# A combination written over its own source, paired residual loads and stores on SyncE in a one-core encoder layer

## The chip, the core and the metric

The kernel runs on one core of one Trainium2 chip. The metric is the device time of one launch in microseconds. The kernel before takes 855.76 us (median of three runs, 854.52 to 856.06). The engines are named as the profile names them: PE (TensorE matmul; PEld is its weight load), DVE (VectorE), ACT (ScalarE), POOL (GpSimd) and SP (SyncE, which here only issues DMAs). SPq and POOLq are the instruction streams of SP and POOL.

## The reference, cut to what matters

The reference is one encoder layer on x of 1024 positions by 1024 channels: a Fourier token mixer, then a gated MLP with a 3-tap convolution over positions, each with adaLN modulation before it and a residual and LayerNorm behind it.

```python
h = modulate(x, sh1, sc1)
y = fourier_mixer(h, w_out)                      # real part of fft2, then a linear map
x = layer_norm(ALPHA * x + g1 * y, mix_g, mix_b) # kept in HBM as x1d

h = modulate(x, sh2, sc2)
u = h @ w_up                                     # 1024 -> 2 * 2816
u = conv3_over_positions(u) + conv_b
val, gate = u[:, :2816], u[:, 2816:]
y = (gelu(gate) * val) @ w_down                  # 2816 -> 1024
x = layer_norm(ALPHA * x + g2 * y, ffn_g, ffn_b) # the output
```

All tensors are float32.

## The kernel before, in words

Every large matmul is done three times (`hl3`, L282 to L285): both operands are split into a high part (ACT, L52) and a low part (DVE, L53, the source minus its high part), and high times high, high times low and low times high are added in PSUM. So each matmul operand costs one ACT and one DVE instruction before PE can use it.

**Up projection.** The 2816 value and 2816 gate columns are done in 22 blocks `j` of 128 and 128. Blocks 0 and 1 are done plainly (L570 to L620): block 1 has four accumulators `x1_{ph}{v}`, for the two halves `ph` of the positions and for value and gate, written in the order ph 0, then ph 1. From block 2 on, a block is done with seven instead of eight products (a Strassen-Winograd scheme, L624 to L669). On the side of the weights it needs the sums S1 to S4 of the four raw quarters, which POOL makes (L632 to L635) in the tiles `S12_j` (slot 31) and `S34_j` (slot 32). On the side of the positions it needs combinations T1 to T4 of the quarters `B` of the activations (`comb`, L531), made once by DVE and then split: T2 has its raw form in slots 46 and 47, and T4, which is T2 minus a quarter, has its raw form in slots 31 and 32. Slots 31 and 32 hold two weight tiles of block 0 before that, and `S12_2` and `S34_2` after that. T3 is split into the tiles `Hh0` to `Hh3`, over the positions 512 to 1023 of the plain operand, which block 1 reads at ph 1. The result of each block is convolved and gated (`gated`, L572) and stored to HBM (`gd`) by POOL.

**Down projection.** It also has seven products `p`, done in the order 1, 2, 5, 6, 3, 7, 4 (L915), each in six pieces `i` of the contraction: five pieces of two 128-row tiles and one single tile. The g operand of product `p` is read from `gd`, and the w operand from the weights; sums are made by DVE (L747, L762) or by DMAs from POOL that add to what is in the tile (L732, L752, L756). PE adds products in `o{p}_{m}{c}`, one bank for each 128-row block `m` of positions, and `evac` (L808) adds a finished product into the tiles `C[0]` (upper positions) and `C[1]` (lower positions).

**Upper rows.** After products 2 and 3 a half of the columns of the upper rows is complete. For each row block `m` and each half `h` of the columns, `upper_half` (L873) multiplies by the gate (L875) and adds the residual `xu`, a 128x512 piece of x1d that SP loads (`xu_load`, L794). There are two slots for it, 24 and 44, used in turn by m. `upper` and `normed` (L878, L883) then make the LayerNorm: ACT squares (L887), DVE and POOL make the inverse deviation (L423, L425), ACT scales (L891), DVE multiplies by `ffg` (L892) and adds `ffb` (L893), and `store` issues the DMA to the output, from POOL for the upper rows and from SP for the lower rows. The lower rows are done after products 7 and 4 (`lower`, L898, and L825 to L864).

**What sets the order.** PE, DVE and ACT instructions are put in order by the compiler's scheduler from its own estimate; SP and POOL (`manual_schedule`, L924) issue in the order in which the code is written. Every engine works strictly through its own list, so an instruction that waits holds up all behind it. `UL` (L921) says before which step (p, i) an `xu_load` is written, `U0` and `U1` where the halves of the upper rows are written, `XL` where the residual of the lower rows (`xf`) is loaded. Loads of operands run seven steps ahead (L926).

Of the kernel before, what the change touches and what calls it, by code (L numbers as in the profile page):

```python
# [8 lines left out]
F32 = mybir.dt.float32  # L9
F32R = mybir.dt.float32r  # L10
AF = mybir.ActivationFunctionType
ALU = mybir.AluOpType
# [23 lines left out]
def encoder_layer(ctx: ExitStack, tc: tile.TileContext, I, out: bass.AP):  # L36
# [8 lines left out]
    def slot(i, shape, dt, name):  # L45
        return big.tile([128] + list(shape), dt, tag=f"s{i}", name=name)
# [8 lines left out]
    def E(name):  # L55
        return pool if name in ON_POOL else dve
# [371 lines left out]
    for n_t, t in enumerate((1, 2, 0, 3)):  # L428
        ts_ = slice(128 * t, 128 * t + 128)
        xr = []  # L430
# [100 lines left out]
    def comb(name, x, y, op, sl):  # L531
        out_ = []
        for i in range(2):
            v = slot(sl + i, [2, 512], F32, f"{name}_{i}")
            for q in range(2):
                E(name).tensor_tensor(v[:, q, :], x[2 * i + q], y[2 * i + q], op)
                out_.append(v[:, q, :])
        return out_
# [67 lines left out]
    T3 = comb("T3", B[1, 1], B[0, 1], ALU.subtract, 34)  # L606
    T4 = comb("T4", T2, B[1, 0], ALU.subtract, 31)
    gated(0, u0[0], u0[1])
    u1 = [slot((2, 0)[v], [S], F32, f"u1_{v}") for v in range(2)]
    for ph in range(2):  # L610
        for v in range(2):
            g = slice(512 * ph, 512 * ph + 512)
            acc = xbank(f"x1_{ph}{v}")
            plain_mm(acc, a1, v, lambda a: a[:, g])
            act.activation(u1[v][:, g], acc, AF.Copy)
# [176 lines left out]
    xr = {}  # L792

    def xu_load(m, h):  # L794
        v = slot((24, 44)[m % 2], [512], F32, f"xu{m}_{h}")
        sp.dma_start(v, x1d[128 * m : 128 * m + 128, 512 * h : 512 * h + 512])
        xr[0, m, h] = v

# [5 lines left out]
    def store(half, m):  # L804
        r0 = 512 * half + 128 * m
        (pool, sp)[half].dma_start(out[r0 : r0 + 128, :], C[half][m])

# [75 lines left out]
    def normed(half, m, nmu):  # L883
# [9 lines left out]
        E(f"ub{m}").tensor_tensor(c, c, ffb, ALU.add)  # L893
        store(half, m)

# [24 lines left out]
    XL = {(7, 5): (1, 0), (4, 0): (1, 1), (4, 1): (1, 2), (4, 2): (1, 3)}  # L920
    UL = {**{(6, i): (i - 1, 0) for i in range(1, 5)}, **{((7, i) if i else (3, 5)): (i, 1) for i in range(4)}}  # L921
    U0 = {(6, i + 1): i - 1 for i in range(1, 5)}
    U1 = {(7, i + 1): i for i in range(4)}
    ctx.enter_context(tc.manual_schedule(engines={mybir.EngineType.SP, mybir.EngineType.Pool}))  # L924
    for n, (p, i) in enumerate(steps):
# [37 lines left out]
        while split_n < min(len(steps), n + 2):  # L963
            opnd[steps[split_n]] = operands(*steps[split_n], ready.pop(steps[split_n]))
            split_n += 1
        late.append((PAIRS[i], opnd.pop((p, i))))
        if (p, i) in U1:
            upper_half(U1[p, i], 1)
            upper(U1[p, i])
# [122 lines left out]
```

## Time and profile before

| what | value |
|---|---|
| time, three runs | 854.52, 855.76, 856.06 us |
| the profiled execution: time | 853.01 us |
| the profiled execution: span | 851.1 us |
| PE busy (share of the span) | 797.7 us (94%) |
| DVE busy | 702.5 us (83%) |
| ACT busy | 387.0 us (45%) |
| POOL busy | 244.5 us (29%) |
| mean granted clock of PE | 0.976 |
| HBM read, written | 110.39 MB, 19.92 MB |

The span goes from the first to the last instruction of the profiled execution, which is 1.9 us less than that execution's own time; that in turn is 2.75 us below the median of the three runs. The up projection's seven-product blocks fill about 232 to 614 us, the down projection 614 to 830 us, and from 830 us on only LayerNorm and stores are left. In a timeline row the first two numbers are start and duration in us, then engine, line, operation, output<-inputs; in square brackets stands how long the engine sat idle before it and what ended that.

### The profile page before, as it was taken

The page shows a single profiled execution, that of the slowest core. Times are in us where ns is not written, and L with a number is a line of the kernel's source. Part 1 is how long each engine was busy: PE and PEld are TensorE (multiplying, and loading weights), DVE is VectorE, ACT ScalarE, POOL GpSimd, SP SyncE. Part 2 cuts the span into 40 slices and gives each one's busy share as a digit, 9 for nine tenths or more (in the row PEclk, how much of TensorE's full clock was granted, in tenths as well). Part 3 has the DMA queues.
Part 4 walks back from the last instruction along what each step waited for, and adds up shares of the span by engine and source line. Part 5 has one row for each costly group of instructions (what it writes and reads, how often), then busy time and mean ns, then how long its engine had stood idle before and what let it go on. Part 6 is the DMA issues. An engine that isn't in the chain of part 4 may idle for free.

```text
span 851.1 us, 10735 instructions
## 1 busy us (share of the span) xinstructions
PE 797.7 (94%) x3943; PEld 643.7 (76%) x3943; DVE 702.5 (83%) x1030; ACT 387.0 (45%) x559; POOL 244.5 (29%) x205
## 2 busy tenths in 40 slices
PE   2899999878999999999999999999999989999990
PEld 1566768667878888888888888888878878888880
DVE  7959677888799999998888888888677784557897
ACT  7634435565733444444444443444354334335611
POOL 2162013230064433444433334331000122702203
PEclk9999999988999999999999999999999999999995
DMA  9987843821113122222222222210598887988903
GB/s 343 363 296 244 327 171 124 322 100 49 50 58 116 74 87 108 102 76 75 75 94 82 97 87 87 74 50 25 200 376 301 270 229 127 193 159 237 292 26 124
DMA packets 50613, 133.90 MB, mean 157 GB/s; under 512 B 5608, under 2 KB 6760, under 8 KB 50560
## 3 DMA queue, kind: packets, MB, share of 16 engines
q1 hardware_dynamic: 39504, 103.59, 34.1%
q0 software_dynamic: 10768, 28.58, 13.7%
q10 hardware_dynamic: 288, 1.05, 0.3%
q8 instruction: 31, 0.51, 0.2%
q14 instruction: 22, 0.18, 0.1%
HBM read 110.39 MB, written 19.92 MB: 153 GB/s over the span
## 4 chain that ended last, share of the span: by engine, by line
PE 74%; DVE 11%; DMA 9%; issue 3%; ACT 2%; POOL 1%; SPq 0%; POOLq 0%; DVEq 0%; ACTq 0%
PE x L284 16%; PE x L285 16%; PE x L283 16%; PE o L284 4%; PE o L285 4%; PE o L283 4%; DMA xu<-x1d 4%; PE ada L135 2%; DMA gr<-gd 2%; DMA wd<-in_w_down_dram 1%; PE B L283 1%; DVE d_1l L53 1%; PE B L285 1%; PE B L284 1%; DVE d_0l L53 1%
## 5 line engine op out<-in xcount | busy, mean ns | idle before, releaser
L283 PE MATMUL x<-Hh,a 128*128 128x512 f32 (+2 forms) x416 | 157.3, 380 | 4.2 <-ACT Hh L52 4.2
L284 PE MATMUL x<-Hl,a 128*128 128x512 f32 (+2 forms) x416 | 157.0, 379 | 1.8 <-DVE Hl L53 1.8
L285 PE MATMUL x<-Hh,a 128*128 128x512 f32 (+2 forms) x416 | 155.7, 376 | 0.9 <-DVE a L53 0.9
L284 PE MATMUL o<-d_1l,d_0h 128*128 128x512 f32 (+1 forms) x299 | 114.8, 385 | 3.1 <-DVE d_1l L53 3.1
L285 PE MATMUL o<-d_1h,d_0l 128*128 128x512 f32 (+1 forms) x299 | 114.3, 384 | 0.0
L283 PE MATMUL o<-d_1h,d_0h 128*128 128x512 f32 (+1 forms) x299 | 102.8, 383 | 0.0
L283 PEld LDWEIGHTS x<-Hh,a 128*128 128x128 f32 x416 | 79.9, 193 | 19.6 <-ACT Hh L52 5.1
L284 PEld LDWEIGHTS x<-Hl,a 128*128 128x128 f32 x416 | 79.4, 191 | 18.1 <-DVE Hl L53 3.9
L285 PEld LDWEIGHTS x<-Hh,a 128*128 128x128 f32 x416 | 79.4, 191 | 15.1 <-DVE a L53 1.3
L52 ACT ACTIVATE a<-S 128x512 fp32r<-128x512 f32 x80 | 49.9, 628 | 85.4 <-PE x L285 70.5
L284 PEld LDWEIGHTS o<-d_1l,d_0h 128*128 128x128 f32 x299 | 56.7, 190 | 15.2 <-DVE d_1l L53 4.1
L285 PEld LDWEIGHTS o<-d_1h,d_0l 128*128 128x128 f32 x299 | 56.7, 189 | 10.9
L283 PEld LDWEIGHTS o<-d_1h,d_0h 128*128 128x128 f32 x299 | 56.2, 188 | 11.0
L53 DVE TENSOR_TENSOR a<-S,a 128x512 fp32r<-128x512 f32 x80 | 60.6, 758 | 2.8 <-ACT a L52 2.2
L53 DVE TENSOR_TENSOR a<-wu,a 128x512 fp32r<-128x512 f32 x60 | 62.1, 1037 | 0.0
L587 POOL DMA_DIRECT2D gd<-ug x20 | 11.5, 573 | 170.4 <-DVE ug L586 170.4
L52 ACT ACTIVATE a<-wu 128x512 fp32r<-128x512 f32 x60 | 37.3, 624 | 33.2 <-PE x L285 33.2
L634 POOL TENSOR_TENSOR S<-wu 128x512 f32<-128x512 f32 x20 | 28.1, 1406 | 63.1 <-DVE a L53 57.2
L578 DVE SCALAR_TENSOR_TENSOR t<-uv,cw,t 128x1023 f32<-128x1023 f32 x20 | 34.6, 1731 | 11.6 <-ACT t L577 11.5
L53 DVE TENSOR_TENSOR d_1l<-wd,d_1h 128x1024 fp32r<-128x1024 f32 (+1 forms) x37 | 44.0, 1189 | 0.0
L635 POOL TENSOR_TENSOR S<-wu,S 128x512 f32<-128x512 f32 x20 | 43.9, 2193 | 0.1
L52 ACT ACTIVATE d_0h<-Sg 128x1024 fp32r<-128x1024 f32 x15 | 15.9, 1061 | 56.6 <-PE o L284 56.6
(317 smaller groups left out, 1839.2 us busy)
## 6 DMA issues: line engine op xcount, KB each, us to landing
aw<-in_ada_w_dram SPq DMA_DIRECT2D x48, 512.0 KB, 6.8
wu<-in_w_up_dram SPq DMA_DIRECT2D x44, 512.0 KB, 3.2
gd<-ug POOLq DMA_DIRECT2D x20, 512.0 KB, 2.9
wd<-in_w_down_dram SPq DMA_DIRECT2D x20, 512.0 KB, 10.8
gr<-gd SPq DMA_DIRECT2D x15, 512.0 KB, 7.1
gA<-gd SPq DMA_DIRECT2D x10, 512.0 KB, 9.7
Sg<-gd POOLq DMA_DIRECT2D x10, 512.0 KB, 6.4
x<-in_x_dram SPq DMA_DIRECT2D x8, 512.0 KB, 7.3
```

The costliest lines, as they stand in the source:

```text
L52: act.activation(hi, src, AF.Copy)
L53: (eng or dve).tensor_tensor(lo, src, hi, ALU.subtract)
L135: pe.matmul(pm[32 * g : 32 * g + 32, :], cb[:, kt, :], ws[kt][:, q * g : q * g + q], start=(kt == 0), stop=(kt == KT - 1), tile_position=( ...
L283: pe.matmul(ps_ap, hi_l, hi_r, start=first, stop=False)
L284: pe.matmul(ps_ap, hi_l, lo_r, start=False, stop=False)
L285: pe.matmul(ps_ap, lo_l, hi_r, start=False, stop=last)
L578: dve.scalar_tensor_tensor(tt[:, 1:S], u[:, 0 : S - 1], w[:, 0:1], tt[:, 1:S], ALU.mult, ALU.add)
L587: pool.dma_start(gd[j], gg)
L634: pool.tensor_tensor(S3, A11, A21, ALU.subtract)
L635: pool.tensor_tensor(S4, A12, S2, ALU.subtract)
```

## The change

It has three parts.

1. T4 is written over T2's raw tiles (slots 46 and 47) instead of into slots 31 and 32 (`comb` with `None` as slot), and block 1 of the up projection does positions 512 to 1023 (ph 1) before 0 to 511 (ph 0).
2. The residual of the upper rows is loaded as four pieces of 256 rows by 512 columns (one DMA of 512 KB for two row blocks), not eight of 128 rows. Slot 24 has the row blocks 0 and 1, slot 44 the row blocks 2 and 3. `UL` puts the loads of the first column half at steps (2, 5) and (5, 0) instead of (6, 1) to (6, 4), and those of the second half at (3, 1) and (3, 2) instead of (3, 5) and (7, 1) to (7, 3).
3. The upper rows are stored by SP at steps (4, 0) to (4, 3), not by POOL behind each row's LayerNorm.

```diff
--- before.py
+++ after.py
@@ -531,10 +531,11 @@
     def comb(name, x, y, op, sl):
         out_ = []
         for i in range(2):
-            v = slot(sl + i, [2, 512], F32, f"{name}_{i}")
+            v = slot(sl + i, [2, 512], F32, f"{name}_{i}") if sl is not None else None
             for q in range(2):
-                E(name).tensor_tensor(v[:, q, :], x[2 * i + q], y[2 * i + q], op)
-                out_.append(v[:, q, :])
+                o = x[2 * i + q] if v is None else v[:, q, :]
+                E(name).tensor_tensor(o, x[2 * i + q], y[2 * i + q], op)
+                out_.append(o)
         return out_
 
     cw = cp.tile([128, NB, 2, 4], F32, name="cw")
@@ -604,10 +605,10 @@
     t_op("T2", 1, T2)
     t_op("T1", 0, T1)
     T3 = comb("T3", B[1, 1], B[0, 1], ALU.subtract, 34)
-    T4 = comb("T4", T2, B[1, 0], ALU.subtract, 31)
+    T4 = comb("T4", T2, B[1, 0], ALU.subtract, None)
     gated(0, u0[0], u0[1])
     u1 = [slot((2, 0)[v], [S], F32, f"u1_{v}") for v in range(2)]
-    for ph in range(2):
+    for ph in (1, 0):
         for v in range(2):
             g = slice(512 * ph, 512 * ph + 512)
             acc = xbank(f"x1_{ph}{v}")
@@ -791,10 +792,11 @@
     C = [[slot(c, [D], F32, f"C{hf}_{m}") for m, c in enumerate(sl)] for hf, sl in enumerate(((0, 1, 4, 5), (2, 6, 7, 3)))]
     xr = {}
 
-    def xu_load(m, h):
-        v = slot((24, 44)[m % 2], [512], F32, f"xu{m}_{h}")
-        sp.dma_start(v, x1d[128 * m : 128 * m + 128, 512 * h : 512 * h + 512])
-        xr[0, m, h] = v
+    def xu_load(q, h):
+        v = slot((24, 44)[q], [2, 512], F32, f"xu{q}_{h}")
+        sp.dma_start(v, x1d[256 * q : 256 * q + 256, 512 * h : 512 * h + 512].rearrange("(m p) n -> p m n", p=128))
+        for m in range(2):
+            xr[0, 2 * q + m, h] = v[:, m, :]
 
     def x_load(half, m):
         xr[half, m] = slot((24, 44, 47, 48)[m], [D], F32, f"xf{half}_{m}")
@@ -803,7 +805,7 @@
 
     def store(half, m):
         r0 = 512 * half + 128 * m
-        (pool, sp)[half].dma_start(out[r0 : r0 + 128, :], C[half][m])
+        sp.dma_start(out[r0 : r0 + 128, :], C[half][m])
 
     def evac(p, m, x):
         c0, c1 = C[0][m], C[1][m]
@@ -891,7 +893,6 @@
         act.activation(c, c, AF.Identity, scale=rs, bias=nb)
         E(f"ug{m}").tensor_tensor(c, c, ffg, ALU.mult)
         E(f"ub{m}").tensor_tensor(c, c, ffb, ALU.add)
-        store(half, m)
 
     st1 = []
 
@@ -918,7 +919,7 @@
     TAIL = {3: 2, 7: 2, 4: 4}
     acc, late = None, []
     XL = {(7, 5): (1, 0), (4, 0): (1, 1), (4, 1): (1, 2), (4, 2): (1, 3)}
-    UL = {**{(6, i): (i - 1, 0) for i in range(1, 5)}, **{((7, i) if i else (3, 5)): (i, 1) for i in range(4)}}
+    UL = {(2, 5): (0, 0), (5, 0): (1, 0), (3, 1): (0, 1), (3, 2): (1, 1)}
     U0 = {(6, i + 1): i - 1 for i in range(1, 5)}
     U1 = {(7, i + 1): i for i in range(4)}
     ctx.enter_context(tc.manual_schedule(engines={mybir.EngineType.SP, mybir.EngineType.Pool}))
@@ -964,6 +965,8 @@
             opnd[steps[split_n]] = operands(*steps[split_n], ready.pop(steps[split_n]))
             split_n += 1
         late.append((PAIRS[i], opnd.pop((p, i))))
+        if p == 4 and i < 4:
+            store(0, i)
         if (p, i) in U1:
             upper_half(U1[p, i], 1)
             upper(U1[p, i])
```

Line numbers of the changed kernel are one higher than before from L538 on, and two higher in the later functions.

**SP, where the down projection's product 5 begins.** `wd11` are the weights that product 6 needs, `xu` the residual pieces (row block or pair, then column half), `gr13` and later the g operand of product 7. Before:

```order
L686 DMA wd11_0_5778<-in_w_down_dram 128x2x512
L686 DMA wd11_2_5817<-in_w_down_dram 128x2x512
L686 DMA wd11_4_5852<-in_w_down_dram 128x2x512
L686 DMA wd11_6_5888<-in_w_down_dram 128x2x512
L686 DMA wd11_8_5924<-in_w_down_dram 128x2x512
L686 DMA wd11_10_5958<-in_w_down_dram 128x512
L796 DMA xu0_0_6026<-x1d_66 128x512
L796 DMA xu1_0_6062<-x1d_66 128x512
L796 DMA xu2_0_6100<-x1d_66 128x512
L796 DMA xu3_0_6138<-x1d_66 128x512
L694 DMA gr13_6204<-gd_67 128x2x512
```

With the change:

```order
L797 DMA xu0_0_5752<-x1d_66 128x2x512
L687 DMA wd11_0_5778<-in_w_down_dram 128x2x512
L797 DMA xu1_0_5781<-x1d_66 128x2x512
L687 DMA wd11_2_5819<-in_w_down_dram 128x2x512
L687 DMA wd11_4_5854<-in_w_down_dram 128x2x512
L687 DMA wd11_6_5890<-in_w_down_dram 128x2x512
L687 DMA wd11_8_5926<-in_w_down_dram 128x2x512
L687 DMA wd11_10_5960<-in_w_down_dram 128x512
L695 DMA gr13_6198<-gd_67 128x2x512
L695 DMA gr14_6238<-gd_67 128x2x512
L797 DMA xu0_1_6242<-x1d_66 128x2x512
```

The first pair now stands ahead of all six weight loads and the second ahead of five of them; the second column half stands behind the second of product 7's loads, where it stood behind the sixth (outside these rows).

**POOL, at the first seven-product block (j = 2).** `u0_1` is the gated result of block 0. Before:

```order
L587 DMA gd_67<-u0_1_1824 128x1024
L634 TENSOR_TENSOR S34_2_2348<-wu2_0_2343 128x512
L632 TENSOR_TENSOR S12_2_2347<-wu2_0_2343,wu2_1_2345 128x512
L633 TENSOR_TENSOR S12_2_2347<-S12_2_2347,wu2_0_2343 128x512
L635 TENSOR_TENSOR S34_2_2348<-wu2_1_2345,S12_2_2347 128x512
L632 TENSOR_TENSOR S12_3_2494<-wu3_0_2490,wu3_1_2492 128x512
```

With the change:

```order
L635 TENSOR_TENSOR S34_2_2346<-wu2_0_2341 128x512
L633 TENSOR_TENSOR S12_2_2345<-wu2_0_2341,wu2_1_2343 128x512
L634 TENSOR_TENSOR S12_2_2345<-S12_2_2345,wu2_0_2341 128x512
L588 DMA gd_67<-u0_1_1824 128x1024
L636 TENSOR_TENSOR S34_2_2346<-wu2_1_2343,S12_2_2345 128x512
L633 TENSOR_TENSOR S12_3_2492<-wu3_0_2488,wu3_1_2490 128x512
```

The store of block 0 was ahead of all four sums of block 2, and is now behind three of them.

**DVE, upper rows against the end.** `pg` is product 4's result times the gate, the first step of the lower rows' end; `C0_2` and `C0_3` are the last two upper row blocks. The part of the list in which the last of their instructions stood, before:

```order
L831 TENSOR_TENSOR pg0_6860<-o4_00_6708,g2_5146 128x512
L912 BN_STATS stl3_6828<-C1_3_5299 128x6 x2
L831 TENSOR_TENSOR pg1_6896<-o4_10_6709,g2_5146 128x512
L832 SCALAR_TENSOR_TENSOR C1_0_5296,stl0_6756<-pg0_6860,C1_0_5296 128x512
L892 TENSOR_TENSOR C0_3_5295<-C0_3_5295,ffg_6462 128x1024
L832 SCALAR_TENSOR_TENSOR C1_1_5297,stl1_6801<-pg1_6896,C1_1_5297 128x512
L834 TENSOR_SCALAR nmuf40_6864<-stl0_6756 128x1
L831 TENSOR_TENSOR pg2_6932<-o4_20_6710,g2_5146 128x512
L893 TENSOR_TENSOR C0_3_5295<-C0_3_5295,ffb_6464 128x1024
L834 TENSOR_SCALAR nmuf41_6900<-stl1_6801 128x1
L843 TENSOR_TENSOR pg3_6989<-o4_30_6711,g2_5146 128x256
```

Where all of the upper rows' last instructions stand with the change, between the splits for products 7 and 4 (`d7`, `d4`):

```order
L894 TENSOR_TENSOR C0_0_5290<-C0_0_5290,ffg_6456 128x1024
L53 TENSOR_TENSOR d7_0l3_6512<-gr16_6314,d7_0h3_6511 128x1024
L895 TENSOR_TENSOR C0_0_5290<-C0_0_5290,ffb_6458 128x1024
L53 TENSOR_TENSOR d7_1l3_6516<-wd00_6_5316,d7_1h3_6515 128x1024
L53 TENSOR_TENSOR d4_0l1_6700<-gA22_1_6452,d4_0h1_6699 128x1024
L894 TENSOR_TENSOR C0_1_5291<-C0_1_5291,ffg_6456 128x1024
L894 TENSOR_TENSOR C0_2_5292<-C0_2_5292,ffg_6456 128x1024
L894 TENSOR_TENSOR C0_3_5293<-C0_3_5293,ffg_6456 128x1024
L895 TENSOR_TENSOR C0_1_5291<-C0_1_5291,ffb_6458 128x1024
L53 TENSOR_TENSOR d7_0l4_6563<-gr17_6350,d7_0h4_6562 128x1024
L53 TENSOR_TENSOR d4_1l1_6704<-wd01_2_5382,d4_1h1_6703 128x1024
L895 TENSOR_TENSOR C0_2_5292<-C0_2_5292,ffb_6458 128x1024
```

The four instructions of `C0_2` and `C0_3` with `ffg` and `ffb`, two of which stood among the `pg` rows and two between product 7's end and them, now stand ahead of product 7's end.

## The prediction

> **What bounds the kernel now.** I read the page first: the span, and the busy tenths of the engines by slice of 21.3 us.
>
> ```profile
> span 851.1 us, 10735 instructions
> PE   2899999878999999999999999999999989999990
> DVE  7959677888799999998888888888677784557897
> PEclk9999999988999999999999999999999999999995
> ```
>
> PE is full from the second slice to the last but one, so time can be won only where PE is not full or its clock drops, and behind its last matmul. The view by stretches says how much that is at the three places that the change touches (PE, PEld, DVE, ACT and POOL busy with counts, then granted clock, DMA share, GB/s).
>
> ```profile
> 240.00:250.00 10.00, 9.10 (x41) 7.20 (x40) 10.00 (x12) 3.37 (x5) 5.64 (x4) 1.00 0.29 107
> 680.00:700.00 20.00, 17.74 (x71) 14.15 (x71) 17.42 (x25) 6.03 (x6) 3.77 (x4) 0.91 0.87 222
> 820.00:851.00 31.00, 10.51 (x60) 9.09 (x58) 26.77 (x51) 4.97 (x7) 8.13 (x7) 0.72 0.25 103
> ```
>
> So: 0.9 us without PE at 241, 2.3 us and a lower clock in product 5 of the down projection, and an end in which DVE works 26.8 of 31 us. The other holes of PE (the start, and 180 to 210) lie ahead of the first instruction that moves, and I leave them as they are.
>
> **Part 1, T4 over T2: +1.2 us.** Timelines of PE, POOL, ACT and SP around 240, and how long the `wu` loads of that stretch took to land:
>
> ```profile
> 240.33 0.39 PE L284 MATMUL x<-TT1l,a 128*128 128x512 f32 x1
> 241.62 0.50 PE L285 MATMUL x<-Hh,a 128*128 128x512 f32 x1 [0.90 <-DVE a L53]
> 233.17 1.53 POOL L634 TENSOR_TENSOR S<-wu 128x512 f32<-128x512 f32 x1 [5.85 <-ACT u L615]
> 237.12 1.67 POOL L632 TENSOR_TENSOR S<-wu,wu 128x512 f32<-128x512 f32 x1 [2.42 <-DVE TT4l L53]
> 238.87 2.14 POOL L633 TENSOR_TENSOR S<-S,wu 128x512 f32<-128x512 f32 x1
> 234.16 0.57 ACT L655 ACTIVATE p<-x 128x512 f32<-128x512 f32 x1
> 220.55 0.33 SPq L549 DMA_DIRECT2D wu<-in_w_up_dram  x1
> DMA to landing us min/median/max: 3.1/4.1/4.7
> ```
>
> POOL's sums for block 2 start at 233 and 237, because S34 and S12 take the slots that T4 leaves only when it is split. Matmuls stand 0.227 us apart where nothing waits, so the one at 241.62 should have come at 240.56: 1.1 us, and 0.1 more as the next ones run slower. With the change slots 31 and 32 are free when block 0's last weights are read. What is late next is the second half of block 2's weights, issued at 220.55: with 4.7 us it is there at 225.3, S1 and S2 (1.67 and 2.14) at 229.1, and their splits (0.6 on ACT and DVE each) at 230.4. PE finishes product 0 about 234.1 and wants the operand of product 1 from 231.8 on. S3 and S4 are made by 232.5, and PE wants them ten microseconds later. That leaves 1.4 us of cover. If the splits are held up by more (DVE is full here), a wait comes back. Ends: -0.5 and +1.2; I take 1.2. The T4 subtractions are as many as before, and the turned order of block 1 has the same matmuls; it lets T3's splits, which overwrite positions 512 to 1023, start before block 1 ends.
>
> **Part 2, the residual pairs, at product 5: +3.2 us.** PE, DVE and SP there:
>
> ```profile
> 686.39 1.07 PE L283 MATMUL o<-d_1h,d_0h 128*128 128x512 f32 x4
> 689.72 0.50 PE L284 MATMUL o<-d_1l,d_0h 128*128 128x512 f32 x1 [2.26 <-DVE d_1l L53]
> 696.01 1.07 PE L283 MATMUL o<-d_1h,d_0h 128*128 128x512 f32 x4
> 701.45 1.07 PE L283 MATMUL o<-d_1h,d_0h 128*128 128x512 f32 x4
> ```
>
> ```profile
> 673.94 1.22 DVE L747 TENSOR_TENSOR wd<-wd,wd 128x1024 f32<-128x1024 f32 x1 [0.64 <-DMA wd<-in_w_down_dram]
> 686.08 0.69 DVE L876 SCALAR_TENSOR_TENSOR C<-xu,C 128x512 f32<-128x512 f32 x1 [0.91 <-DMA xu<-x1d]
> 688.45 1.22 DVE L53 TENSOR_TENSOR d_1l<-wd,d_1h 128x1024 fp32r<-128x1024 f32 x1
> 667.27 4.28 SPq L686 DMA_DIRECT2D wd<-in_w_down_dram  x6
> 671.85 17.03 SPq L796 DMA_DIRECT2D xu<-x1d  x4
> wd<-in_w_down_dram SPq DMA_DIRECT2D x20, 512.0 KB, 10.8
> ```
>
> A piece takes PE 701.45 - 696.01 = 5.44 us; this one took 9.62, so the hole costs 4.2 us: 2.26 of waiting and 1.9 at a lower clock. DVE is late with `d_1l` because it waits 0.91 us for `xu` and has a full list. [...]
>
> With the change the first pair is issued where the first `wd` was, so it lands about when that did, 673.9, and does not hold DVE up. But the weights come later. From the first `wd` at 673.9 to the `xu` at 686.1 the loads brought 2.25 MB of weights and 0.25 MB of `xu`: 4.9 us per MB. The first `wd` follows one pair (0.5 MB): 676.3; the last follows both: 689.7. DVE can begin at 673.7, when product 2's first rows are done, and by its new order has 1.75 us of work ahead of the first `wd` (two of 0.6 per 128x512, one of 1.14 per 128x1024): ready 675.9, so it waits 0.4. From there to the end of `d_1l` are four instructions of 1.14 and ten of 0.6 and one more 1.14: 688.0, against PE's 687.5. Then it wants the last `wd` at 688.0, and gets it at 689.7; piece 3's `d_1l` ends at 693.8 where PE comes at 693.5. Left are 0.8 us of waits with a little slow clock: 4.2 - 1.0 = 3.2. The pair's own size has no row; loads of that size (`wu` above from 3.1 us on, `wd` 10.8 in the median) bound it, and give 4.2 and 0 here. The early load of the second half meets nobody: it takes the place of DMAs at 771 to 784.
>
> **Parts 2 and 3, the end: +3.3 us.** DVE's groups from 806 on, then its timeline and PE's:
>
> ```profile
> L892 DVE TENSOR_TENSOR C<-C,ffg 128x1024 f32<-128x1024 f32 x2 | 2.4, 1214 | 0.0
> L893 DVE TENSOR_TENSOR C<-C,ffb 128x1024 f32<-128x1024 f32 x2 | 2.4, 1210 | 0.0
> 778.12 0.69 DVE L876 SCALAR_TENSOR_TENSOR C<-xu,C 128x512 f32<-128x512 f32 x1 [4.91 <-DMA xu<-x1d]
> 806.08 0.68 DVE L823 TENSOR_TENSOR C<-C,o 128x512 f32<-128x512 f32 x1
> 846.23 1.28 DVE L863 SCALAR_TENSOR_TENSOR C<-C,rsf,ffb 128x1024 f32<-128x1024 f32 x1 [0.44 <-POOL rsf L850]
> 769.45 0.39 PE L283 MATMUL o<-d_1h,d_0h 128*128 128x512 f32 x1
> 802.62 0.39 PE L285 MATMUL o<-d_1h,d_0l 128*128 128x512 f32 x1
> ```
>
> Product 7 starts on PE at 769.45, and its first row block is complete at 803.0. DVE takes it at 806.1, 3.1 us late, since it lost 4.9 us at 773 to 778 waiting for `xu`. From 806.1 to 847.5 it works without a hole of over 0.5 us: the end is DVE's list, and the upper rows' last four instructions are in it. With the change `xu` is there long before, and the list has those four (4 x 1.14 = 4.6 us) ahead of product 7's end, where DVE waited. PE's new order has 12 more matmuls ahead of that end, half narrow (2.0 us): DVE starts at 805.0 in the old clock, 1.1 us sooner. One split of 1.14 comes into the stretch. And PE now waits for DVE in it: 18 instructions of 0.6 and four of 1.14 stand before product 4's piece 3 is split (15.4 us), and PE has matmuls for 12.0, so the first finished row of product 4 comes at 21.0 to 22.7 us (slow clock) where DVE is at 20.9. I take 1.2 for it. 4.6 + 1.1 - 1.1 - 1.2 = 3.3; ends 1 and 5.
>
> The stores go from POOL to SP at like cost (us from issue to landing at the line's end), and SP has nothing urgent behind them but the residual of the lower rows, which is used 15 us later. I cost them at nothing.
>
> ```profile
> out_dram<-C POOLq DMA_DIRECT2D x4, 512.0 KB, 3.0
> out_dram<-C SPq DMA_DIRECT2D x4, 512.0 KB, 2.6
> ```
>
> **A new wait in product 7: -1.0 us.** DVE now has the four small products with POOL's result (`nbfn`, L892 of the new kernel) ahead of splits that PE needs, and POOL has its own list ahead of them:
>
> ```profile
> 771.50 0.33 SPq L694 DMA_DIRECT2D gr<-gd  x1
> 777.68 0.88 POOL L732 DMA_DIRECT2D gr<-gd  x1 [7.24 <-DMA gr<-gd]
> 784.25 1.47 POOL L425 TENSOR_TENSOR rs_fn<-ve_fn,mhalf 128x1 f32<-128x1 f32 x1 [4.45 <-DVE ve_fn L423]
> 794.57 1.24 POOL L756 DMA_DIRECT2D wd<-in_w_down_dram  x1 [0.43 <-issue]
> 795.34 1.32 POOL L425 TENSOR_TENSOR rs_fn<-ve_fn,mhalf 128x1 f32<-128x1 f32 x1
> gr<-gd POOLq DMA_DIRECT2D x5, 512.0 KB, 17.4
> ```
>
> Before, POOL waited for the rows (4.45); now the rows wait for POOL. The last g load of product 7 is issued when DVE frees its slot, 2.7 us into the product (2.1 before), and lands 6.2 us later: 8.9. POOL then issues two DMAs and makes the first power by 11.1, and one more in each 2.1 us (a DMA and a power), the fourth 1.3 behind the third: 16.6. Behind it DVE has eleven instructions of 1.14 to the split of product 4's piece 1: 29.2. PE gets there after 128 matmuls, seven of them narrow: 28.3. I take 1.0 us of lost time; ends 0 and 2.5.
>
> **Rivals.** (a) *Weights late.* The six `wd` queue behind 1 MB of residual, and if they take 10.8 us each time rather than share the way they did, product 5 keeps its whole hole: part 2's 3.2 us are gone, 852.3. For it: the DMA share was 0.87 there. Against: the first pair replaces traffic that came just behind. [...] (b) *The end does not shrink.* The four moved instructions only push DVE's splits, DVE is late for product 7's end as before, and the last 3.3 us stay: 852.4. For it: with the moved instructions DVE's list in product 7 is longer, and waits for POOL stand in it. Against: it lost 4.9 us there before and still did nearly all of it. (c) *Slower.* The chain load, POOL, `nbfn`, DVE, PE: each microsecond by which the last g load lands later than 8.9 goes to PE in full. If it takes the 17.4 us of POOL's own `gr` transfers instead of 6.2, that is 11.2 us more: 860. It is slower than before from some 8.4 us on, so from a landing 14.6 us behind the issue. For it: all loads of product 4 now follow it without a pause. Against: they stand behind it in the queue. (d) *Nothing happens*: an edit that the list shows but another wait covers everywhere, 855.8. I see no such wait.
>
> **How the numbers follow.** 1.2 + 3.2 + 3.3 - 1.0 = 6.7 us. The profiled execution's 853.0 would become 846.3; the median of the runs lies 2.75 us above it, and 855.8 becomes **849.1**. Chances: the forecast (845 to 852) 0.64, (a) 0.12, (b) 0.13, (c) 0.07, (d) 0.04. Good ends of all terms together (1.2 + 4.2 + 5 - 0) would give 845.4, so the range begins at 845; it goes up to 854, where (a) and (b) alone are inside and (c), (d) and (a) with (b) are left out. A measurement of this kernel tells about 0.2% (1.7 us) from no change. Faster by more: the forecast, and most of (a) and (b): 0.82. Within: (d) and the rest of (a) and (b), 0.10. Slower: 0.08.
>
> **What would show it.** Right: no idle PE at 241 and POOL's first sum of block 2 near 216; product 5's piece under 6.5 us; DVE without a wait for `xu`; nothing with `ffg` on a C[0] tile behind product 7; the last matmul to the last DVE instruction 15 us or less, where it was 17. Wrong: `wd` named as what DVE waits for in product 5 with over 2 us (a), DVE starting product 7's end over 2 us behind PE (b), or waits of DVE for `rs_fn` of more than 8 us in all (c).

## The result and the profile after

The changed kernel takes 848.33 us (median of four runs, 848.1 to 850.46) where the kernel before takes 855.91 us in the runs beside it: ratio 0.9924, 95% interval 0.9903 to 0.9945, so 4.7 to 8.3 us less, 6.5 in the middle. Forecast were 849.1 us and 6.7 us less. The profiled execution took 848.1 us; its span and the busy tenths by slice:

```profile
span 846.3 us, 10731 instructions
PE   2899999878999999999999999999999999999983
DVE  6959778887999999888888888888678794557997
PEclk9999999997999999999999999999999999999997
```

The view by stretches, at the three places shown of before:

```profile
240.00:250.00 10.00, 10.00 (x46) 8.28 (x45) 10.00 (x13) 3.64 (x7) 3.71 (x3) 1.00 0.30 107
680.00:700.00 20.00, 19.56 (x85) 15.60 (x84) 18.44 (x26) 8.03 (x8) 4.51 (x4) 1.00 1.08 320
820.00:846.00 26.00, 12.29 (x64) 10.42 (x62) 19.68 (x39) 3.73 (x6) 5.08 (x4) 0.76 0.20 82
```

PE has no hole near 241 any more, 0.4 us instead of 2.3 in product 5, and is still at work after 830, where it had stopped. **Early.** POOL's first two sums of block 2, from its timeline; they started at 233 and 237 before:

```profile
216.53 2.40 POOL L635 TENSOR_TENSOR S<-wu 128x512 f32<-128x512 f32 x1 [21.32 <-PE x L285]
225.78 1.39 POOL L633 TENSOR_TENSOR S<-wu,wu 128x512 f32<-128x512 f32 x1 [6.84 <-DMA wu<-in_w_up_dram]
```

**Product 5.** PE's rows at the piece that took 9.62 us, and DVE's one wait there; then how long after their issue product 6's weights landed (the trace has the landing of four of the six), of before and (second fence) of the changed kernel:

```profile
685.90 1.07 PE L283 MATMUL o<-d_1h,d_0h 128*128 128x512 f32 x4
687.40 0.50 PE L284 MATMUL o<-d_1l,d_0h 128*128 128x512 f32 x1 [0.44 <-DVE d_1l L53]
692.08 1.07 PE L283 MATMUL o<-d_1h,d_0h 128*128 128x512 f32 x4
688.87 0.69 DVE L748 TENSOR_TENSOR wd<-wd,wd 128x512 f32<-128x512 f32 x1 [1.52 <-DMA wd<-in_w_down_dram]
```

```profile
DMA to landing us min/median/max: 10.5/12.5/12.9
```

```profile
DMA to landing us min/median/max: 13.0/16.1/16.6
```

The piece now takes 692.08 - 685.90 = 6.18 us, though the weights land 2.5 to 3.7 us later behind their issue than before: DVE waits for the last of them, behind the split that PE needs, and no longer for `xu`.

**The end.** DVE's and PE's rows of the changed kernel from product 7 on:

```profile
777.27 0.16 DVE L892 TENSOR_TENSOR nbfn<-nmufu,rs_fn 128x1 f32<-128x1 f32 x1 [3.33 <-POOL rs_fn L425]
801.97 0.69 DVE L825 TENSOR_TENSOR C<-C,o 128x512 f32<-128x512 f32 x1 [0.66 <-PE o L285]
813.63 0.28 PE L283 MATMUL o<-d_1h,d_0h 128*128 128x256 f32 x1
816.21 1.22 DVE L53 TENSOR_TENSOR d_1l<-wd,d_1h 128x1024 fp32r<-128x1024 f32 x1
817.48 0.50 PE L284 MATMUL o<-d_1l,d_0h 128*128 128x512 f32 x1 [3.57 <-DVE d_1l L53]
818.96 0.63 PE L283 MATMUL o<-d_1h,d_0h 128*128 128x512 f32 x1
821.93 0.40 PE L284 MATMUL o<-d_1l,d_0h 128*128 128x512 f32 x1
841.42 1.28 DVE L865 SCALAR_TENSOR_TENSOR C<-C,rsf,ffb 128x1024 f32<-128x1024 f32 x1
```

DVE is now at product 7's end before PE has it (0.66 us of waiting; it came 3.1 us late before). But in product 4 PE waits 3.57 us for a split, and the twelve matmuls behind it take 821.93 - 817.48 = 4.45 us, where 2.7 would do at the 0.227 us at which matmuls follow each other when nothing waits. So PE's last matmul comes at 832.0, 1.8 us later than before, and the time from there to DVE's last instruction falls from 17.3 to 10.7 us.

To compare kernels by stage, four landmarks serve, and only distances between them are compared: the last wait in the plain blocks of the up projection (202.22 before, 204.03 changed), the first matmul of product 1 (614.79, 615.18), product 5's pieces (above), and the row at which DVE takes product 6's first result, before and changed:

```profile
737.69 0.69 DVE L818 TENSOR_TENSOR C<-C,o 128x512 f32<-128x512 f32 x1 [2.89 <-PE o L285]
```

```profile
734.02 0.69 DVE L820 TENSOR_TENSOR C<-C,o 128x512 f32<-128x512 f32 x1 [2.89 <-PE o L285]
```

| stage, us | before | changed | less by | forecast |
|---|---|---|---|---|
| up to the plain blocks | 202.22 | 204.03 | -1.8 | 0 |
| from there to product 1 | 412.57 | 411.15 | 1.4 | 1.2 |
| products 1, 2 and half of 5 | 71.60 | 70.72 | 0.9 | 0 |
| product 5's two pieces | 15.06 | 11.88 | 3.2 | 3.2 |
| from product 6's first result to DVE's last instruction | 109.82 | 108.68 | 1.1 | 2.3 |

The rows add up to the 4.8 us between the two spans; the stretch between the fourth and the fifth row takes 36.24 us in both. The first and the third row belong to instructions that the change does not move, and had to be told from spread.

### The profile page after: what moved, and what is told of

It reads as the page before. It is cut to its first block, busy times and chain, and to the rows that moved or that the text cites. A ratio compares the mean times of both kernels' runs of the same rounds, so it can differ in the third digit from the quotient of the medians.

```text
span 846.3 us, 10731 instructions
## 1 busy us (share of the span) xinstructions
PE 797.2 (94%) x3943; PEld 644.0 (76%) x3943; DVE 701.3 (83%) x1030; ACT 387.9 (46%) x559; POOL 238.1 (28%) x201
## 3 DMA queue, kind: packets, MB, share of 16 engines
q10 hardware_dynamic: 288, 1.05, 0.3%
## 4 chain that ended last, share of the span: by engine, by line
PE 87%; DVE 8%; issue 2%; DMA 1%; POOL 1%; ACT 0%; SPq 0%; DVEq 0%; ACTq 0%
PE x L284 17%; PE x L285 17%; PE x L283 17%; PE o L284 7%; PE o L285 7%; PE o L283 7%; PE ada L135 2%; PE B L283 1%; PE B L285 1%; PE B L284 1%; PE trm L486 1%; DMA aw<-in_ada_w_dram 1%; PE A L285 1%; PE A L284 1%; PE A L283 1%
## 5 line engine op out<-in xcount | busy, mean ns | idle before, releaser
L284 PEld LDWEIGHTS o<-d_1l,d_0h 128*128 128x128 f32 x299 | 56.5, 189 | 16.6 <-DVE d_1l L53 5.6
L53 DVE TENSOR_TENSOR a<-wu,a 128x512 fp32r<-128x512 f32 x60 | 61.4, 1023 | 0.0
L588 POOL DMA_DIRECT2D gd<-ug x20 | 11.5, 573 | 176.3 <-DVE ug L587 153.5
L53 DVE TENSOR_TENSOR a<-S,a 128x512 fp32r<-128x512 f32 x80 | 57.4, 717 | 0.9
```

The costliest lines, as they stand in the source:

```text
L53: (eng or dve).tensor_tensor(lo, src, hi, ALU.subtract)
L284: pe.matmul(ps_ap, hi_l, lo_r, start=False, stop=False)
L588: pool.dma_start(gd[j], gg)
```

## The experiments

All fourteen profiles by the same landmarks; the ratio is to the kernel before in runs on the same chip. "Early" is the second row of the table above, "pieces" the fourth (in brackets PE's hole in it), "end" the fifth.

| kernel | median us | ratio (95%) | early | pieces (hole) | end |
|---|---|---|---|---|---|
| before | 855.91 | | 412.57 | 15.06 (2.26) | 109.82 |
| before, again | 855.75 (one run) | | 412.90 | 15.50 (2.70) | 110.62 |
| changed | 848.33 | 0.9924 (0.9903-0.9945) | 411.15 | 11.88 (0.44) | 108.68 |
| changed, again | 845.91 (one run) | | 411.04 | 11.84 (0.51) | 108.26 |
| part 1 alone | 851.72 | 0.9966 (0.9947-0.9984) | 411.06 | 16.08 (3.27) | 109.67 |
| part 1 without the turned order | 851.8 (one run) | | 411.36 | 13.97 (2.77) | 110.91 |
| part 2 alone | 847.71 | 0.9916 (0.9894-0.9937) | 412.53 | 14.95 (2.16) | 105.44 |
| part 3 alone | 857.08 | 1.0028 (1.0011-1.0045) | 412.50 | 15.91 (3.14) | 111.03 |
| parts 1 and 2 | 846.57 | 0.9895 (0.9877-0.9914) | 411.04 | 13.24 (2.07) | 105.93 |
| the same, `xu` ahead of all loads | 855.61 | 1.0001 (0.9986-1.0017) | 419.92 | 12.52 (1.34) | 105.44 |
| the same as parts 1 and 2, second pair behind | 847.63 | 0.9918 (0.9886-0.9950) | 411.48 | 15.15 (2.52) | 105.45 |
| changed, first half late | 851.06 | 0.9948 (0.9927-0.9969) | 411.05 | 13.80 (2.62) | 109.73 |
| changed, splits first | 845.60 | 0.9886 (0.9863-0.9910) | 411.23 | 12.22 (1.05) | 106.51 |
| the same, second pair behind | 848.99 | 0.9925 (0.9900-0.9950) | 411.15 | 15.79 (2.96) | 106.04 |

### The kernel before, once more

No edit.

> The kernel before once more, for the spread of the stages. Theory 1: the stages that no moved instruction touches differ between two profiles of one kernel by as much as between before and after: the start up to the first plain matmul of the up projection (202.2 us before, 204.0 after) comes out anywhere from 202 to 204.5, while the hole at 241 (0.9 us) and product 5's slow piece (9.6 us) come back within 0.3 us. Rival: the start is 202.2 within 0.3 us, and then the change made the start 1.8 us longer. The 0.5 us hole of product 1 near 638: if it is absent here, product 1's gain is spread and not the change.

The start came out at 204.18 us, 2 us later than in the first profile; over all kernels it lies between 201.8 and 205.7. Product 1's hole of 0.54 us near 638 is absent here, and present again in three profiles of other kernels (0.4 to 0.6). So the first and the third row of the stage table are spread. The hole at 241 (0.86) and product 5's hole (2.70) came back; the piece with that hole took 10.06 us, 0.44 more than in the first profile, where 0.3 were expected at most.

### Part 1 alone

```diff
-    T4 = comb("T4", T2, B[1, 0], ALU.subtract, 31)
+    T4 = comb("T4", T2, B[1, 0], ALU.subtract, None)
...
-    for ph in range(2):
+    for ph in (1, 0):
```

> Only part 1 (T4 over T2's tiles and block 1 done ph 1 first). Theory 1, each part acts in its own stage: PE has no hole at 241 us, the stretch from the first matmul of the plain blocks to product 1 of the down projection is 1.4 us shorter (412.6 us before, 411.2 in the changed kernel), and everything from there on stands as before: a small hole in product 1 near 638, product 5's slow piece at 9.6 us, 17 us from the last matmul to DVE's last instruction. Time 1.2 to 1.6 us below the kernel before. Rival, part 1 also gives what product 1 gained: the hole of 0.5 us near 638 is gone too and the time is 2.3 us lower.

The early stretch is 411.06 us, the hole at 241 is gone, product 5 and the end are as before, and product 1's hole is there (0.64 us): theory 1. The interval of the ratio is 1.4 to 4.5 us: its middle is more than the stage explains, but the stage's 1.5 us lies inside it.

### Part 1 without the turned order

```diff
-    T4 = comb("T4", T2, B[1, 0], ALU.subtract, 31)
+    T4 = comb("T4", T2, B[1, 0], ALU.subtract, None)
```

> The kernel before with T4 over T2's tiles, but block 1 still in the order ph 0, ph 1. Theory 1, the free slots alone do it: POOL's first sum of block 2 starts near 216, no hole at 241, and the stretch from the plain blocks to product 1 is 411.1 us as with all of part 1. Rival, the turned order carries a part of it, since T3's splits overwrite the positions that ph 1 reads: the stretch is 411.7 us or more, with a wait of PE near 230 to 245.

411.36 us, and POOL's first sum at 214.91: the free slots do it. The 0.3 us to the kernels with both edits lie within the spread of these stretches (411.04 to 411.48).

### Part 2 alone

```diff
-    UL = {**{(6, i): (i - 1, 0) for i in range(1, 5)}, **{((7, i) if i else (3, 5)): (i, 1) for i in range(4)}}
+    UL = {(2, 5): (0, 0), (5, 0): (1, 0), (3, 1): (0, 1), (3, 2): (1, 1)}
```

(with `xu_load` in pairs as in the change)

> Only part 2 (residual in pairs, loaded earlier; upper rows still stored by POOL behind their LayerNorm). Theory 1: product 5's two pieces take 11.9 us instead of 15.1 (3.2 us), DVE waits nowhere for xu, and in the list three of the four upper row blocks are finished ahead of product 7's end, so the tail behind the last matmul is some 13 us instead of 17. Hole at 241 as before. Time 4 to 5.5 us below before. Rival, the end's gain needs the stores on SP: the end is as long as before or longer (POOL's stores hold up the weights' adding DMAs and with them product 4), and the time is 3 us lower or less.

The end is 105.44 us, 4.4 less than before and 3.2 less than in the changed kernel, with POOL's stores in place: the rival is wrong, and theory 1 is right there. In product 5 theory 1 failed, since the pieces hardly gained in this profile (14.95). Part 2 alone is as fast as the whole change (847.71 and 848.33 us), by 5.4 to 9.1 us under the kernel before. The end and product 5 are both looked at below.

### Part 3 alone

```diff
-        (pool, sp)[half].dma_start(out[r0 : r0 + 128, :], C[half][m])
+        sp.dma_start(out[r0 : r0 + 128, :], C[half][m])
...
-        store(half, m)
...
+        if p == 4 and i < 4:
+            store(0, i)
```

> Only part 3 (upper rows stored by SP at product 4). Theory 1, stores cost nothing by themselves: product 5 stays at 15.1 us, DVE still waits about 5 us for xu in product 7, and since the upper rows' last instructions now all stand ahead of product 7's end in a list that lost those 5 us, DVE is later for product 7's end and PE waits in product 4 by 5 us or more; the tail is shorter by about as much. Time within 1.5 us of before. Rival, the SP stores alone free POOL and shorten the end: 2 us or more faster.

Slower, by 0.9 to 3.8 us: the rival is wrong. DVE's longest waits in product 7, then PE in product 4:

```profile
DVE C L876 <- DMA xu<-x1d: 6.2, 3, 5.3
DVE nbfn L890 <- POOL rs_fn L425: 1.2, 3, 0.5
```

```profile
823.55 0.50 PE L284 MATMUL o<-d_1l,d_0h 128*128 128x512 f32 x1 [3.89 <-DVE d_1l L53]
```

PE waits 3.89 us in product 4, where theory 1 had 5 or more, and the time from the last matmul to DVE's last instruction falls by 5.3 us (17.3 to 12.0). The hole in product 4 thus stands here too, and in no kernel without part 3 is it over 0.4 us: part 3 brings it.

### Parts 1 and 2 without part 3

```diff
-        sp.dma_start(out[r0 : r0 + 128, :], C[half][m])
+        (pool, sp)[half].dma_start(out[r0 : r0 + 128, :], C[half][m])
...
+        store(half, m)
...
-        if p == 4 and i < 4:
-            store(0, i)
```

> Parts 1 and 2 together, without part 3: the upper rows are stored by POOL as before. Theory 1, part 3 costs time at the end, since with POOL's list free of stores the compiler puts all upper rows' last instructions ahead of product 7's end and product 4's last splits too late for PE: here there is no hole in product 4 and from product 6's last results to DVE's last instruction it takes 105.4 us as with part 2 alone (108.7 in the changed kernel, 109.8 before). Time 844 to 846.5, some 3 us below the changed kernel. Rival, the end does not depend on who stores: 108 us or more, time 847.5 to 849.5.

The end is 105.93 us and product 4 has no hole. What the stores change can be read on POOL. The changed kernel, where it issues the adding loads of product 4's weights one after the other; then this kernel, where two of them stand behind stores that wait for DVE:

```profile
776.34 2.09 POOL L757 DMA_DIRECT2D wd<-in_w_down_dram  x1
777.62 2.30 POOL L757 DMA_DIRECT2D wd<-in_w_down_dram  x1
```

```profile
785.00 0.61 POOL L808 DMA_DIRECT2D out_dram<-C  x1 [6.29 <-DVE C L895]
786.03 1.23 POOL L757 DMA_DIRECT2D wd<-in_w_down_dram  x1 [0.42 <-issue]
794.79 0.60 POOL L808 DMA_DIRECT2D out_dram<-C  x1 [6.27 <-DVE C L895]
795.39 0.91 POOL L757 DMA_DIRECT2D wd<-in_w_down_dram  x1
```

With the stores off POOL, the compiler puts more of product 4's matmuls on PE ahead of product 7's end (twelve of those with 256 columns instead of six at most), and on DVE the last upper row and more of the lower rows' first instructions ahead of product 4's last splits. That the earlier weights are its reason is likely, but no run shows it. Whether this order is what costs, the next experiment tells. The time, 846.57 us, is at the upper edge of theory 1's range, 1.8 us under the changed kernel's in the median. But the intervals overlap, and from the plain blocks on the two first profiles are equally long (642.2 and 642.3 us): this kernel lost in products 1 and 5 what it won at the end.

### The changed kernel, product 4's splits first

```diff
-        if p == 4 and 0 <= i - 1 < 4:
-            lower(i - 1)
...
+        if (p, i) == (4, 4):
+            with tc.issue_after(lo_ins[4, 3]):
+                for m in range(4):
+                    lower(m)
```

(`lo_ins[4, 3]` is the low split of product 4's fourth weight piece; the edge sets the order and adds no wait)

> The changed kernel, with the lower rows' multiplications and residual additions in DVE's list behind the split of product 4's fourth piece (an order edge, no wait). Theory 1, the hole of 3.57 us in product 4 and the lower clock behind it (5.4 us together) come from those instructions standing ahead of the split: here the hole is under 0.5 us, PE's last matmul 4.5 to 5.5 us earlier, and the end 1.5 to 3 us shorter, since DVE is then what ends last. Rival, DVE's amount of work sets the end whatever its order: PE is earlier but the time from product 6's last results to the end stays at 108.7 within 0.7 us, the time the same within 1 us.

The stretch from 805 to 825 us, of the changed kernel and of this one (PE, PEld, DVE, ACT, POOL busy, granted clock, DMA share, GB/s):

```profile
805.00:825.00 20.00, 16.43 (x78) 13.74 (x77) 18.02 (x32) 4.95 (x6) 0.00 (x0) 0.91 0.01 1
```

```profile
805.00:825.00 20.00, 20.00 (x106) 17.19 (x105) 19.26 (x33) 4.95 (x6) 0.00 (x0) 1.00 0.01 1
```

PE is full at full clock, its last matmul comes 5.1 us sooner after product 6 (92.9 us instead of 98.0), and the end is 106.5 us instead of 108.3 to 108.7. So the order alone made the hole, and the hole and the low clock behind it, 5.3 us of PE (3.57, and 1.73 in the twelve matmuls), cost some 2 us of time, since DVE has its own list to finish. Of all kernels this one has the lowest median, 845.6 us. It beats the kernel before clearly; that it beats the changed kernel is read from the stage, the intervals overlap.

### The changed kernel, once more

No edit.

> The changed kernel once more, for the spread of its stages. Theory 1: the hole of 3.57 us in product 4 belongs to the list and comes back within 0.5 us; product 5's two pieces (11.9 us in the first profile) depend on when the weights land and come out anywhere from 11 to 15; the start up to the first plain matmul 202 to 204.5. Rival: product 5's gain is fixed, 11.9 within 0.3 us, and the part-2 profile with 15 us was an exception that only that kernel has.

The hole in product 4 is back with 3.56 us, and the pieces take 11.84. Against theory 1, product 5's gain is thus the same in both profiles of this kernel.

### The changed kernel with the first half late

```diff
-    UL = {(2, 5): (0, 0), (5, 0): (1, 0), ...
+    UL = {(6, 1): (0, 0), (6, 3): (1, 0), ...
```

> The changed kernel with the first column half of the residual back where it was, as two pairs behind all six weight loads of product 6; everything else as changed. Theory 1, product 5's gain of the change comes from the early place of the first half: the weights land 12.5 us after their issue again (16.1 in the changed kernel), DVE waits a microsecond or more for xu, product 5's two pieces take 14.5 to 15.5 us (11.9 changed, 15.1 before), the hole of 3.57 us in product 4 stays; time 2.5 to 3.5 us above the changed kernel. Rival, the pairs help by their number alone, wherever they stand: the pieces take 12.5 or less and the time is that of the changed kernel within 1 us.

The pieces take 13.80 us, below the range expected but 1.9 above the changed kernel; DVE waits for `xu` again:

```profile
687.67 0.69 DVE L878 SCALAR_TENSOR_TENSOR C<-xu,C 128x512 f32<-128x512 f32 x1 [1.12 <-DMA xu<-x1d]
```

PE's hole there is 2.62 us, and the one in product 4 is back with 3.57. So in the changed kernel it is the place of the first half, not the number of DMAs, that product 5 gains from. The end is 109.73 us, 1.0 more than in the changed kernel: behind product 4's hole the matmuls stand 0.43 us apart for twelve steps here (820.58 to 825.70) and for eight there (818.53 to 821.93).

### The residual ahead of all loads

```diff
-    UL = {(2, 5): (0, 0), (5, 0): (1, 0), (3, 1): (0, 1), (3, 2): (1, 1)}
+    UL = {(3, 1): (0, 1), (3, 2): (1, 1)}
...
+    xu_load(0, 0)
+    xu_load(1, 0)
     for n, (p, i) in enumerate(steps):
```

(on parts 1 and 2)

> Parts 1 and 2 without part 3, and the first column half of the residual is loaded ahead of all operands of the down projection, in the last blocks of the up projection where the DMA share is 0.1 to 0.2. Theory 1, the weights that product 5 adds up are late because 1 MB of residual stands in the queue with them, by up to 2 us, and by a different amount in each execution: here DVE waits for no wd in product 5 and the two pieces take 11.2 us or less (10.9 is the least); time 0.5 to 2.5 us below the same kernel without it. Rival, DVE's own list sets product 5: the pieces take 11.9 or more though no weight is late, and the time is the same within 0.5 us.

A miss: 9 us slower than without it. SP's first loads and PE's first matmul of product 1 in this kernel, and (second fence) the first load in the one with parts 1 and 2:

```profile
613.01 0.89 SPq L797 DMA_DIRECT2D xu<-x1d  x2
613.94 0.47 SPq L687 DMA_DIRECT2D wd<-in_w_down_dram  x1
623.01 0.80 PE L283 MATMUL o<-d_1h,d_0h 128*128 128x512 f32 x1 [8.68 <-ACT d_0h L52]
```

```profile
598.53 0.38 SPq L687 DMA_DIRECT2D wd<-in_w_down_dram  x1
```

Slots 24 and 44 also hold split operands of the up projection (`T_slots`, L503), up to its last products. SP stood at the pair until 613 with all weights behind it. In product 5 it speaks for the rival: the weights land 6.7 to 12.8 us after their issue, DVE waits 0.66 us for the first of them and for none behind it, and PE's hole is still 1.34 us. So at least half of that hole is left by DVE's own list, in which the last weights' subtraction stands ahead of the split here.

### The second pair behind the weights

```diff
-    UL = {(2, 5): (0, 0), (5, 0): (1, 0), ...
+    UL = {(2, 5): (0, 0), (5, 5): (1, 0), ...
```

On parts 1 and 2:

> Parts 1 and 2 without part 3, with the second pair of the first column half behind product 6's weights instead of ahead of five of them. Theory 1, what is left of product 5's hole there (2.1 us) is the weights' lateness: half a megabyte less ahead of them lets the second one land some 2.5 us sooner, DVE waits under 0.3 us for it, product 5's two pieces take 11 to 11.8 us (13.2 with the pair ahead); the time is 1 to 2 us lower, 844.5 to 846. Rival, the wait only moves to the second pair, which DVE needs ahead of the next split: the pieces take 13 or more and the time is the same within 0.7 us.

And on the changed kernel with the splits first:

> The changed kernel with product 4's splits first, and with the second pair behind product 6's weights. Theory 1, as above: product 5's two pieces 11 to 11.8 us instead of 12.2, the end as in the kernel with the splits first (106.5 us from product 6's last results on); time 0.5 to 1.2 us lower, about 844.7, the fastest of all. Rival, DVE waits for the second pair instead: 12.2 or more, the same time within 0.7 us.

Both are misses: 15.15 and 15.79 us. DVE in the second of them:

```profile
686.58 0.69 DVE L748 TENSOR_TENSOR wd<-wd,wd 128x512 f32<-128x512 f32 x1 [1.88 <-DMA wd<-in_w_down_dram]
687.19 1.22 DVE L53 TENSOR_TENSOR d_1l<-wd,d_1h 128x1024 fp32r<-128x1024 f32 x1
```

DVE doesn't wait for the second pair, as the rival had it, but the compiler has swapped two rows: the subtraction that needs the last weights stands ahead of the split that PE waits for, and its wait of 1.88 us goes to PE (hole 2.96). In the changed kernel the same wait (1.52 us at 688.87) stands behind that split and costs nothing. In the first of the two kernels the same rows are swapped: DVE waits 1.02 us for the first weights and 0.32 us for the last, and the hole is 2.52.

## Why the prediction was right, and where it was not

The forecast was right in sign and size; in two of the three places the mechanism was right too, at the end it was not. By stage, with the means of all profiles that share the stage:

- **Part 1, +1.2: right.** 412.5 to 412.9 us without it, 411.0 to 411.5 with it: 1.5 us. Slots 31 and 32 are the cause, as argued; the cover of 1.4 us for the second half of the weights held.
- **Part 2 in product 5, +3.2: right for the changed kernel (3.2 and 3.2 in two profiles), and less sure than it looked.** With the residual in its old place the pieces take 13.8 to 16.1 us in six profiles, 15.1 in the mean. That the weights come some microseconds later and just fit is what the landing times show (2.5 to 3.7 us). But parts 1 and 2 alone, with the same DVE list there, have 13.24, and part 2 alone 14.95, since their weights land another 0.4 to 2.2 us later (14.9/16.7/17.3 and 15.2/16.6/17.0 us after their issue) and DVE waits for the second of them ahead of the split. In the kernel of parts 1 and 2:

```profile
683.03 1.22 DVE L748 TENSOR_TENSOR wd<-wd,wd 128x1024 f32<-128x1024 f32 x1 [1.59 <-DMA wd<-in_w_down_dram]
```

  Rival (a) is thus real, by that much; why those two kernels have the later weights and the three with part 3 do not is open. And by the author's estimate about 1.6 us of the 3.2 (1.9 of slow matmuls behind the hole of the kernel before, against 0.3 in other kernels) hang on where that hole falls (last section): behind holes of 2.62 and 2.77 us the matmuls stood 0.23 us apart, and against those two profiles the gain is 1.9 and 2.1 us.
- **The end, +3.3 and -1.0: near by luck, with errors that offset each other.** The step "I cost them at nothing" on the stores was wrong, not for SP's or POOL's time, but because without them on POOL the compiler orders DVE and PE otherwise. Part 2 alone shortens the end by 4.8 us (110.3 in the mean of four to 105.4), part 3 takes some 3 of it back (108.3, 108.7, and 109.7 with the first half late). Nor did the gain need all four moved instructions (4.6): with part 2 alone two of them still stand behind product 7's end (at 818.85 and 824.22, the end at 803.95). The other two, and DVE at product 7's end 34.5 us after the product's first matmul instead of 36.6, make the 4.4 us against the first profile. PE's arrival at product 4's fourth piece 12.0 us after product 7's end, and DVE's 15.4, were read rightly from the list (813.75 and 817.34 against 801.97: 11.8 and 15.4). The term that was mis-sized is the price: 1.2 was taken for the stall, and the splits put first give about 2. The wait in product 7 (-1.0) came at the split that was named, but small: POOL's first power is used 11.5 us into the product (forecast 11.1), DVE waits 4.9 us for POOL in all, and PE then waits about 0.1 us for the split, in the second profile not at all. With all three parts the most was 0.50 us, where product 4's splits come first:

```profile
795.16 0.50 PE L284 MATMUL o<-d_1l,d_0h 128*128 128x512 f32 x1 [0.50 <-DVE d_1l L53]
```

- **Sum.** 1.5 + 3.2 + 1.8 (109.8 to 110.9 without the change, 108.3 and 108.7 with it) = 6.5 us, which is also what the ratio gives. With pieces that spread over 2.3 us and ends that spread over 1.2 us in kernels alike there, so close an agreement is luck.
- **Rivals.** (b) is out: DVE waits for product 7's end. (c) is out: 4.9 us of waits for POOL, under the 8 named. (d) is out: the interval of the ratio ends below 1.

## What to carry to other kernels

Taking an instruction out of one engine's list can cost more than it saves when a compiler orders the others by its own estimate, and a change of several parts can hold one that costs: parts 1 and 2 alone have a lower median (846.57 us) than all three (848.33). Read what the list of the engine that ends last looks like afterwards, and where an operand that PE needs stands behind work that nobody waits for, an order edge is worth trying. A wait costs by what stands behind it on its engine: the same 1.5 to 1.9 us for the last weights were free behind a split (1.52 us, a hole of 0.44 in PE) and dear ahead of it (1.88 us, a hole of 2.96). And a load that is issued early must have its slot free early, or it holds up what SP issues behind it: with the residual ahead of all loads the first weights were issued at 613.94 us instead of 598.53.

## What the runs showed of the hardware

A hole of PE does not have one price. In product 5, what the piece takes above its 5.44 us and the hole itself was 0.3 us for all holes up to 2.07 us and 1.9 us for all from 2.96 up; between them it was one or the other, in no order of size: 2.16, 2.26 and 2.70 us cost 1.9 and 2.52 cost 1.7, while 2.62 and 2.77 cost 0.3. The kernel of parts 1 and 2, and (second fence) that of part 2 alone, at the same place:

```profile
685.26 1.07 PE L283 MATMUL o<-d_1h,d_0h 128*128 128x512 f32 x4
688.39 0.50 PE L284 MATMUL o<-d_1l,d_0h 128*128 128x512 f32 x1 [2.07 <-DVE d_1l L53]
693.07 1.07 PE L283 MATMUL o<-d_1h,d_0h 128*128 128x512 f32 x4
```

```profile
686.46 1.07 PE L283 MATMUL o<-d_1h,d_0h 128*128 128x512 f32 x4
689.69 0.50 PE L284 MATMUL o<-d_1l,d_0h 128*128 128x512 f32 x1 [2.16 <-DVE d_1l L53]
695.97 1.07 PE L283 MATMUL o<-d_1h,d_0h 128*128 128x512 f32 x4
```

7.81 and 9.51 us, with holes that differ by 0.09. The granted clock shows where the difference comes from. From 205 us on it changes between 1.00 and 0.50 at 205.61, 690.30, 693.72 and 833.66 us in the trace of the kernel before, and at 207.50, 818.48, 821.89 and 835.55 us in that of the changed kernel; in each of the two these points lie multiples of 3.41 us apart. Views of stretches of that length, first of parts 1 and 2, then of part 2 alone (columns as above):

```profile
683.35:686.77 3.42, 2.98 (x14) 2.12 (x12) 3.42 (x6) 1.54 (x2) 0.00 (x0) 1.00 1.05 404
686.77:690.18 3.41, 1.79 (x8) 1.48 (x9) 2.97 (x6) 0.47 (x1) 1.18 (x1) 1.00 1.05 389
690.18:693.60 3.42, 3.42 (x17) 2.84 (x16) 3.42 (x5) 0.56 (x1) 1.19 (x1) 1.00 1.11 289
```

```profile
687.39:690.81 3.42, 1.26 (x6) 0.95 (x6) 3.14 (x4) 1.04 (x2) 1.18 (x1) 1.00 1.05 392
690.81:694.22 3.41, 3.41 (x10) 2.63 (x9) 3.41 (x7) 0.00 (x0) 0.96 (x1) 0.50 1.08 322
```

With part 2 alone the whole hole of 2.16 us lies in one stretch, and the next stretch runs at clock 0.50; with parts 1 and 2 the clock stays at 1.00, so no change marks the bounds there: counted in such steps they are the author's estimate, and by it the hole of 2.07 us is parted into 0.44 and 1.63. The kernel before and the changed kernel have the same picture. Before, the whole hole of 2.26 us lies in the 3.41 us ahead of 690.30, and the clock is 0.50 from there to 693.72. In the changed kernel the hole of 3.57 us in product 4 is parted into 1.16 and 2.41 at 815.07, 3.41 us ahead of 818.48: the clock is 1.00 behind the first part, and 0.50 from 818.48 to 821.89, behind the second. So in these four traces 2.16, 2.26 and 2.41 us without PE in one stretch came before a stretch at 0.50, and up to 1.63 us before one at 1.00.

In those 3.41 us of the changed kernel the matmuls stand 0.43 us apart, instead of 0.23. The length of a hole alone doesn't tell whether the clock falls: 2.16 us were enough, while behind holes of 2.62 and 2.77 us the matmuls stood 0.23 us apart (from 690.51 with the first half late, from 689.24 in part 1 without the turned order). Where the points lie against the hole differs among the four traces; that the same hole may thus cost one run of a kernel 1.6 us (9.51 - 7.81 - 0.09) more than another is the author's estimate, and no two profiles of one kernel show it.
